# Four residual-and-norm joints of a two-block transformer: two sums of squares in turn, or four sums in one pass

## The chip, the cores and the metric

The kernel runs on one core of a Trainium2 chip, as one program. The metric is device time in microseconds (us) of one execution. Three timed executions of the kernel before took 2606.03, 2606.04 and 2597.53 us, with a median of 2606.03 us. A separate, profiled execution gave the trace from which every row below comes.

## The reference

Two blocks run one after another on 256 latent and 256 context tokens of 1024 features. The first holds two layers (a gated linear attention with grouped attention, then a gated linear recurrence), each followed by a gated feed-forward net; the second holds a latent attention with retention and a state-space layer. What this case is about is the joint between a mixer or a feed-forward net and the norm behind it:

```python
def _rms(x, gain, eps=1e-6):
    y = xf * lax.rsqrt(jnp.mean(xf * xf, axis=-1, keepdims=True) + eps)
    return y * gain

def _modulate(h, shift, scale):
    return h * (1 + scale) + shift

x_lat = x_lat + m_lat[2] * _rms(o_lat @ w_out, norm_post_mix[l])
h_lat = _modulate(_rms(x_lat, norm_pre_ffn[l]), m_lat[3], m_lat[4])
x_lat = x_lat + m_lat[5] * _rms(_swiglu(h_lat, ...), norm_post_ffn[l])
if not last:
    ...   # the same three lines for the context tokens
```

With y the product of a weight and s = m * gain the residual is x + s * y * r, where r is one number per token, the inverse root mean square of y. The next norm needs a second number per token, the inverse root mean square of the new x.

## The kernel before

Features lie on the 128 partitions, in 8 tiles k of 128 features; tokens lie along the free dimension, context tokens first (256), latent tokens behind (256). Each product is three matmuls, because a weight is split into a high part (ACT, line 195) and a low part (DVE, line 196), and so is the normalised input X (high by ACT at line 487, low by DVE at line 492 for even k, and for odd k by ACT at line 489 and POOL at line 490). Lines 205 to 207 are the three matmuls; where 512 tokens pass, the first three weights of a product take context and latent tokens apart, in matmuls of 256 columns.

Four joints have the work in question; the texts call them site 1 to 4:

- site 1: behind the output product of the first mixer (`ew_out`), context and latent;
- site 2: behind the first feed-forward net (`f0_d`), context and latent;
- site 3: behind the output product of the second mixer (`ow_out`), latent alone;
- site 4: behind the second feed-forward net (`f1_d`), latent alone, with the norm for the second block.

At each, and for each of the two token segments, the steps are these. While the product streams, each tile of y is copied out (DVE), squared (ACT, line 70) and summed over its 128 features by a matmul with 32 columns of ones (line 77); tile k writes partitions 32*(k % 4) to 32*(k % 4) + 31 of a PSUM bank (tags pa and pb). At the end the bank is copied (DVE `cp`, line 94), turned to token rows by two matmuls (line 97), and eleven small DVE instructions on 128 x 2 numbers make the inverse root (lines 412 to 420). Two matmuls spread it over partitions again (line 111). Then for 8 tiles DVE forms s * y * r (line 507), POOL or DVE adds it to x (line 508: POOL for k in 0, 1, 3, 4, 6), and the new x is squared and summed like y (lines 70 and 77). A second `cp`, a second turn and a second chain of eleven give the inverse root for the norm, whose 8 tiles follow (lines 486 to 492).

At sites 1 and 2 the last three weights of the product finish their context tokens first, so that the context joint runs beside the latent matmuls.

A scheduler orders each engine's instructions ahead of time; an engine then takes them in that order. Two things besides the joints are put into the same stretches. One is the next block's modulation: 512 KB pieces of `ada_w` are loaded by SP (line 326) into two buffers of the pool `mp` under the tag `mraw`, and PE multiplies them (line 329, two matmuls of 512 columns a piece, to 32-column groups). The other, at site 1, is the preparation of state-space weights: PE spreads small tiles (line 1460), POOL multiplies them (`Ec`, lines 1471 and 1472), PE multiplies the result (line 1479).

## Time and profile before

| what | value |
|---|---|
| timed executions | 2606.03, 2606.04, 2597.53 us |
| profiled execution, its own time | 2601.28 us |
| its span, first to last instruction | 2599.5 us |
| mean granted TensorE clock | 0.962 |
| PE, DVE, ACT, POOL busy | 93%, 58%, 37%, 20% |

The profiled execution lies 4.75 us under the median of the timed ones and inside their spread of 8.5 us. Its own time is 1.8 us more than its span. PE is busy nearly throughout, so a stall of another engine matters only where PE runs out of matmuls that it may do. The four sites are the stretches 415 to 461 us, 895 to 944, 1253 to 1288 and 1474 to 1511.

### The profile page before, as it was taken

The numbers are of one execution on the slowest core, as the hardware profiler recorded it, in microseconds if no ns is written. First come the engines' busy times: TensorE is split into PE (matmuls) and PEld (weight loads), VectorE is DVE, ScalarE is ACT, GpSimd is POOL, SyncE is SP. The second block draws the span as 40 slices with busy tenths as digits, with TensorE's granted clock in tenths as the row PEclk, the third lists the DMA queues.
The fourth block names the chain that finished last, engine by engine and source line by source line (L and its number), as shares of the span: only waits on it lengthen the run. The fifth ranks groups of instructions, "written<-read, shape, count | busy, mean of one in ns | idle before, by whom it ended". The sixth has DMA issues, their size and how long they took to land.

```text
span 2599.5 us, 40143 instructions
## 1 busy us (share of the span) xinstructions
PE 2427.1 (93%) x15813; PEld 1979.1 (76%) x15813; DVE 1513.9 (58%) x2897; ACT 972.1 (37%) x1591; POOL 514.6 (20%) x648
## 2 busy tenths in 40 slices
PE   6999989989889998889999999999999999959999
PEld 5875566768678688889699788556888888628999
DVE  5545436865843466674555552665588744485666
ACT  5523323312222253333444453443423224534443
POOL 2910013763710042330100100110100000260000
PEclk9999999989999999999999999999999999989999
DMA  8326673654543332113665522002365533876564
GB/s 284 116 92 223 242 273 100 166 158 122 153 127 100 104 113 98 59 48 105 255 225 181 194 89 82 17 17 74 111 191 178 170 107 96 185 259 220 154 181 152
DMA packets 162925, 378.05 MB, mean 145 GB/s; under 512 B 24144, under 2 KB 70096, under 8 KB 162608
## 3 DMA queue, kind: packets, MB, share of 16 engines
q1 hardware_dynamic: 159728, 368.27, 44.3%
q0 software_dynamic: 3008, 7.21, 1.4%
q8 instruction: 125, 2.05, 0.3%
q14 instruction: 64, 0.52, 0.1%
HBM read 344.75 MB, written 30.67 MB: 144 GB/s over the span
## 4 chain that ended last, share of the span: by engine, by line
PE 73%; DVE 10%; DMA 6%; POOL 5%; ACT 3%; issue 2%; SPq 1%; POOLq 0%; DVEq 0%; ACTq 0%
PE pl L205 17%; PE pl L206 16%; PE pl L207 16%; PE pm L329 3%; POOL Ec L1471 2%; DMA bc<-s_w 2%; DVE lo L196 2%; PE pl L984 2%; PE pa L77 2%; DMA mcol<-ada_t 1%; POOL Ec L1472 1%; PE pl L279 1%; PE pl L280 1%; PE pl L277 1%; DVE pm L395 1%
## 5 line engine op out<-in xcount | busy, mean ns | idle before, releaser
L195 ACT CAST hi<-raw 128x1024 fp32r<-128x1024 f32 (+4 forms) x393 | 400.2, 1020 | 841.9 <-PE pl L206 640.3
L196 DVE TENSOR_TENSOR lo<-raw,hi 128x1024 fp32r<-128x1024 f32 (+4 forms) x393 | 486.6, 1240 | 341.1 <-ACT hi L195 334.9
L206 PE MATMUL pl<-X,hi 128*128 128x256 f32 (+1 forms) x2032 | 654.2, 323 | 5.9 <-POOL X L490 5.7
L205 PE MATMUL pl<-X,hi 128*128 128x256 f32 (+1 forms) x2032 | 657.6, 326 | 1.6 <-ACT X L487 1.6
L207 PE MATMUL pl<-X,lo 128*128 128x256 f32 (+1 forms) x2032 | 652.1, 322 | 1.5 <-DVE lo L196 1.5
L205 PEld LDWEIGHTS pl<-X,hi 128*128 128x128 f32 x2032 | 395.3, 195 | 39.3 <-issue 9.1
L206 PEld LDWEIGHTS pl<-X,hi 128*128 128x128 f32 x2032 | 395.7, 195 | 37.8 <-POOL X L490 8.6
L207 PEld LDWEIGHTS pl<-X,lo 128*128 128x128 f32 x2032 | 396.2, 195 | 33.4 <-issue 4.9
L205 PE MATMUL pl<-hh,hi 128*128 128x256 f32 (+1 forms) x1071 | 330.0, 309 | 10.7 <-ACT hh L1694 10.6
L206 PE MATMUL pl<-hl,hi 128*128 128x256 f32 (+1 forms) x1071 | 328.4, 307 | 8.5 <-DVE hl L1695 8.3
L207 PE MATMUL pl<-hh,lo 128*128 128x256 f32 (+1 forms) x1071 | 326.8, 306 | 0.0
L205 PEld LDWEIGHTS pl<-hh,hi 128*128 128x128 f32 x1071 | 203.7, 191 | 32.2 <-ACT hh L1694 12.2
L206 PEld LDWEIGHTS pl<-hl,hi 128*128 128x128 f32 x1071 | 204.1, 191 | 20.7 <-DVE hl L1695 10.6
L207 PEld LDWEIGHTS pl<-hh,lo 128*128 128x128 f32 x1071 | 204.4, 191 | 10.4 <-DVE y L1708 0.4
L1471 POOL TENSOR_TENSOR Ec<-PGr,bc 128x576 f32<-128x576 f32 x64 | 102.0, 1609 | 181.4 <-DVE lo L196 84.3
L205 PE MATMUL pl<-M,hi 128*128 128x256 f32 (+1 forms) x416 | 125.9, 305 | 6.9 <-ACT hi L195 5.9
L329 PE MATMUL pm<-mraw,s_cc 128*32 128x512 f32 x576 | 116.0, 606 | 10.3 <-DMA mraw<-ada_w 9.8
L207 PE MATMUL pl<-M,lo 128*128 128x256 f32 (+1 forms) x416 | 123.1, 297 | 1.2 <-DVE lo L196 1.2
L206 PE MATMUL pl<-M,hi 128*128 128x256 f32 (+1 forms) x416 | 123.5, 298 | 0.2 <-DVE M L856 0.2
L1708 DVE TENSOR_TENSOR y<-y,pl 128x256 f32<-128x256 f32 (+1 forms) x86 | 45.2, 526 | 127.2 <-PE pl L207 126.9
L490 POOL TENSOR_TENSOR X<-nt,X 128x256 fp32r<-128x256 f32 x48 | 37.4, 781 | 379.7 <-ACT nt L489 379.7
L395 DVE SCALAR_TENSOR_TENSOR pm<-mcol,mrow 128x512 f32<-128x512 f32 x128 | 89.3, 698 | 36.1 <-DMA mcol<-ada_t 22.4
(515 smaller groups left out, 3757.7 us busy)
## 6 DMA issues: line engine op xcount, KB each, us to landing
mraw<-mod_w SPq DMA_DIRECT2D x96, 512.0 KB, 5.5
raw<-f_u SPq DMA_DIRECT2D x88, 512.0 KB, 3.8
mraw<-ada_w SPq DMA_DIRECT2D x64, 512.0 KB, 6.3
raw<-p_u SPq DMA_DIRECT2D x64, 512.0 KB, 3.6
raw<-p_d SPq DMA_DIRECT2D x64, 512.0 KB, 3.6
raw<-ow_fm SPq DMA_DIRECT2D x32, 512.0 KB, 3.3
mcol<-ada_t SPq DMA_DIRECT2D x64, 256.0 KB, 3.1
raw<-f_d SPq DMA_DIRECT2D x32, 448.0 KB, 3.3
```

The lines of the kernel that those rows point to most:

```text
L77: K.nc.tensor.matmul(self.ps[32 * j:32 * j + 32, :N], K.ones[:rows, :32], self.sq[:rows, :N], start=k < 4, stop=k + 4 >= self.kt, skip_gro ...
L195: nc.scalar.copy(hi, raw)
L196: nc.vector.tensor_tensor(lo, raw, f32(hi), ALU.subtract)
L205: mm(out, w[0][:, kw, wsl], xh, start=first and a == 0, stop=False, skip_group_check=True)
L206: mm(out, w[0][:, kw, wsl], xl, start=False, stop=False, skip_group_check=True)
L207: mm(out, w[1][:, kw, wsl], xh, start=False, stop=last and a == nk - 1, skip_group_check=True)
L329: nc.tensor.matmul(ps[32 * j:32 * j + 32, :], s[:, k, :], raw[:, jj * 512:(jj + 1) * 512], start=k == 0, stop=k == KT - 1, skip_group_chec ...
L395: nc.vector.scalar_tensor_tensor(self.psum("pm"), buf[:, n % 2], 1.0, s[:, v], ALU.mult, ALU.mult, accum_out=(dst if h else part)[:, v, j: ...
L490: nc.gpsimd.tensor_tensor(lo[:, k, a:b], t, f32(hi[:, k, a:b]), ALU.subtract)
L984: nc.tensor.matmul(ps[:, :nk], q[:, tt * P:(tt + 1) * P], k[:, :nk], start=True, stop=True)
L1471: nc.gpsimd.tensor_tensor(Ec[i], ff[i], cs[i], ALU.mult)
L1708: nc.vector.tensor_tensor(y[:, c, a0:b0], y[:, c, a0:b0], ps, ALU.add)
```

## The change

A class `Sums` takes the place of two `Squares` at each of the four sites. As soon as a tile of y is there, it forms four products of 256 tokens: y squared, (s*y) squared, s*y*x and x squared (three by ACT, one by DVE), in one buffer of 4 x 256 numbers, and four matmuls sum them into the four 32-partition groups of one bank, both token segments in the same bank side by side. From the four sums per token the two inverse roots follow: r as before, and the mean square of the new x as S(x,x) + r*(2*S(s*y,x) + r*S(s*y,s*y)), without forming the new x. That chain has eleven, four and eleven small DVE instructions, in one piece. Both roots are spread by four matmuls into one bank, and then each tile gets its residual and, right behind it, its norm. The squares of the new x, their matmuls, the second `cp` and the second turn are gone. In the profile's terms, a segment of a site loses 8 ACT squares and 8 sum matmuls of x and gains 16 ACT squares, 8 DVE products and 24 sum matmuls in the stream of the product. `early` (site 2) puts the context norm beside the latent stream too.

The buffer of `Sums` is taken from the pool `mp` under the tag `mraw`, two buffers.

```diff
+class Sums:
+    def add(self, k, t0, t1):
+        K, nc = self.K, self.K.nc
+        for v, a, b in self.segs:
+            if t0 <= a and b <= t1:
+                self.flush()
+                w = K.mp.tile([P, 4, 256], F32, tag="mraw", name=K.n("sums"), bufs=2)
+                x, y, s = self.x[:, k, a:b], self.y[:, k, a:b], self.Pv[:, v, k:k + 1]
+                nc.scalar.activation(w[:, 0], y, AF.Square)
+                nc.scalar.activation(w[:, 1], y, AF.Square, scale=s)
+                nc.vector.scalar_tensor_tensor(w[:, 2], y, s, x, ALU.mult, ALU.mult)
+                nc.scalar.activation(w[:, 3], x, AF.Square)
+                self.last = w, k, a, b
+    def flush(self):
...
+        for q in range(4):
+            K.nc.tensor.matmul(self.ps[32 * q:32 * q + 32, a:b], K.ones[:, :32], w[:, q], start=first, stop=k == KT - 1,
+                               skip_group_check=True)
+    def rstds(self, i, tag):
...
+        v.tensor_copy(cp[:, :n], self.ps[:, a:b])
+        p2 = K.psum(tag)
+        for t in range(nt):
+            nc.tensor.matmul(p2[:, 4 * t:4 * t + 4], cp[:, t * P:(t + 1) * P], vw(K.ident, 0, [[32, 4]]), start=True,
+                             stop=True)
+        s = [vw(p2, q, [[4, nt]]) for q in range(4)]
...
+        K.rstd_rows(s[0], D, nt, r[0])
+        v.tensor_tensor(u, s[1], r[0], ALU.mult)
+        v.scalar_tensor_tensor(u, s[2], 2.0, u, ALU.mult, ALU.add)
+        v.tensor_tensor(u, u, r[0], ALU.mult)
+        v.tensor_tensor(u, s[3], u, ALU.add)
+        K.rstd_rows(u, D, nt, r[1])
...
-    def halves(self, x, y, accs, vecs):
-        new = self.squares(SEGS)
-        Pv, Av, shift = vecs()
-        c, l = SEGS[:1], SEGS[1:]
-        self.residual_scaled(x, y, Pv, c, [accs[0].rstd()], new)
+    def halves(self, sums, vecs, early):
+        Av, shift = vecs()
+        x = sums.x
+        X = self.norm_tiles(T) if early else None
+        by, bx = sums.rstds(0, "pa")
+        for k in range(KT):
+            self.residual(sums, 0, by, k)
+            if early:
+                self.norm_scaled(X, x, Av, shift, SEGS[:1], [bx], (k,))
         yield
-        bl = accs[1].rstd()
-        bc = new[0].rstd()
-        self.residual_scaled(x, y, Pv, l, [bl], new[1:])
-        X = self.norm_tiles(T)
-        bl = new[1].rstd()
-        self.norm_scaled(X, x, Av, shift, c, [bc])
-        self.norm_scaled(X, x, Av, shift, l, [bl])
+        ly, lx = sums.rstds(1, "pb")
+        if not early:
+            X = self.norm_tiles(T)
+            self.norm_scaled(X, x, Av, shift, SEGS[:1], [bx])
+        for k in range(KT):
+            self.residual(sums, 1, ly, k)
+            self.norm_scaled(X, x, Av, shift, SEGS[1:], [lx], (k,))
         yield X
...
-                acc = K.residual_rms(xl, y, K.vecP(m1[:, :, 2], g[:, 1, 1]), LSEG, acc)
-                X = K.norm_mod(xl, K.vecA(m1[:, :, 4], g[:, 1, 2], "b"), m1[:, :, 3], LSEG, acc)
+                X = K.norm_tiles(LAT)
+                Av = K.vecA(m1[:, :, 4], g[:, 1, 2], "b")
+                by, bx = acc.rstds(0, "pa")
+                for k in range(KT):
+                    K.residual(acc, 0, by, k)
+                    K.norm_scaled(X, xl, Av, m1[:, :, 3], LSEG, [bx], (k,))
```

The scheduler's order changes in several places. In the rows below the line numbers are those of the kernel they come from; the new lines 145, 158, 171, 174 and 188 are the DVE product, the sum matmuls, `cp`, the turn and the spreading of `Sums`; 564 and 565 are the old 507 and 508; 550, 554 and 556 the old 486, 490 and 492; 269 to 271 the old 205 to 207; 390 and 393 the old 326 and 329; 1532, 1533 and 1552 the old 1471, 1472 and 1491.

DVE at site 2, before, where the latent tokens' second copy (cp_7527) stands, after the latent residual and ahead of the context norm (pa_7473 holds the context's inverse root):

```order
L508 TENSOR_TENSOR x<-x,nt_7506 128x256
L507 SCALAR_TENSOR_TENSOR nt_7518<-y_3623,vecP_7277,pb_7449 128x256
L508 TENSOR_TENSOR x<-x,nt_7518 128x256
L94 COPY cp_7527<-pb_7479 128x256
L486 SCALAR_TENSOR_TENSOR nt_7550<-x,vecA_7279,pa_7473 128x256
L412 TENSOR_SCALAR ms_7533<-pb_7529 128x2
L486 SCALAR_TENSOR_TENSOR nt_7554<-x,vecA_7279,pa_7473 128x256
L415 TENSOR_SCALAR ms_7535<-ms_7533 128x2
```

DVE at the same place in the changed kernel, where the latent copy (cp_7603) stands (pa_7445 holds both of the context's inverse roots):

```order
L564 SCALAR_TENSOR_TENSOR nt_7495<-y_3666,vecP_3667,pa_7445 128x256
L550 SCALAR_TENSOR_TENSOR nt_7498<-x,vecA_7397,pa_7445 128x256
L564 SCALAR_TENSOR_TENSOR nt_7502<-y_3666,vecP_3667,pa_7445 128x256
L565 TENSOR_TENSOR x<-x,nt_7502 128x256
L556 SCALAR_TENSOR_TENSOR X_7400<-nt_7498,m_95,X_7399 128x256
L550 SCALAR_TENSOR_TENSOR nt_7505<-x,vecA_7397,pa_7445 128x256
L171 COPY cp_7603<-pa_7043 128x256
L476 TENSOR_SCALAR ms_7610<-pb_7605 128x2
```

Before, the context norm is woven into the latent tokens' second chain; in the changed kernel the latent tokens' only chain of 26 begins behind all 8 context tiles (residual and norm).

PE at site 2, before, from the last sums of y on (mraw are pieces of `ada_w`, rs the inverse roots, pb_7479 the sums of the new x):

```order
L77 MATMUL pb_6996<-sq_7426,ones 32x256
L329 MATMUL pm_7974<-mraw_8095,s_cc_459 32x512
L97 MATMUL pb_7431<-pack_sb,cp_7429 128x1 x2
L97 MATMUL pa_7455<-pack_sb,cp_7453 128x1 x2
L329 MATMUL pm_7974<-mraw_8095,s_cc_459 32x512
L329 MATMUL pm_7974<-mraw_8099,s_cc_459 32x512 x2
L111 MATMUL pb_7449<-pack_sb,rs_7434 128x128 x2
L77 MATMUL pb_7479<-sq_7480,ones 32x256
```

PE at the same place in the changed kernel, from the last sums on:

```order
L158 MATMUL pa_7043<-sums_7594,ones 32x256 x4
L188 MATMUL pa_7445<-pack_sb,rs_7411 128x128 x2
L393 MATMUL pm_8060<-mraw_8061,s_cc_459 32x512
L269 MATMUL pl_7742<-X_7399,hi_7738 128x256
L269 MATMUL pl_7805<-X_7399,hi_7801 128x256
L270 MATMUL pl_7742<-X_7400,hi_7738 128x256
L271 MATMUL pl_7742<-X_7399,lo_7739 128x256
L270 MATMUL pl_7805<-X_7400,hi_7801 128x256
L271 MATMUL pl_7805<-X_7399,lo_7802 128x256
L269 MATMUL pl_7868<-X_7399,hi_7864 128x256
L270 MATMUL pl_7868<-X_7400,hi_7864 128x256
L393 MATMUL pm_8060<-mraw_8061,s_cc_459 32x512
```

Before, six pieces of `ada_w` are worked on in site 1's stretch, six in site 2's and four later. In the changed kernel none is in site 1's; the first of all stands right behind site 2's last sums, twelve of the sixteen are spread among the matmuls of the next three weights (pl_7742, pl_7805, pl_7868), two stand around the fourth weight and two later.

POOL at site 1, before, from the first state-space product behind the first norm tiles (X_3526) on:

```order
L1471 TENSOR_TENSOR Ec_3877<-PGr,bc_3860 128x576
L1472 TENSOR_TENSOR Ec_3876<-Ec_3876,Ec_3877 128x576
L490 TENSOR_TENSOR X_3526<-nt_3582,X_3525 128x256
L1471 TENSOR_TENSOR Ec_3936<-PGr,bc_3860 128x576
L490 TENSOR_TENSOR X_3526<-nt_3591,X_3525 128x256
L1471 TENSOR_TENSOR Ec_3937<-PGr,bc_3860 128x576
L1472 TENSOR_TENSOR Ec_3936<-Ec_3936,Ec_3937 128x576
L490 TENSOR_TENSOR X_3526<-nt_3600,X_3525 128x256
L490 TENSOR_TENSOR X_3526<-nt_3609,X_3525 128x256
L1491 DMA tt<-band_3794 16x8x128
L490 TENSOR_TENSOR X_3526<-nt_3618,X_3525 128x256
```

POOL at site 1 in the changed kernel, up to the last norm tile (nt_3661):

```order
L554 TENSOR_TENSOR X_3569<-nt_3646,X_3568 128x256
L565 TENSOR_TENSOR x<-x,nt_3651 128x256
L1552 DMA tt<-band_3992 16x8x128
L1532 TENSOR_TENSOR Ec_4050<-PGr,bc_4034 128x576
L1532 TENSOR_TENSOR Ec_4051<-PGr,bc_4034 128x576
L1532 TENSOR_TENSOR Ec_4110<-PGr,bc_4034 128x576
L1533 TENSOR_TENSOR Ec_4050<-Ec_4050,Ec_4051 128x576
L1532 TENSOR_TENSOR Ec_4111<-PGr,bc_4034 128x576
L1533 TENSOR_TENSOR Ec_4110<-Ec_4110,Ec_4111 128x576
L1532 TENSOR_TENSOR Ec_4179<-PGr,bc_4163 128x576
L554 TENSOR_TENSOR X_3569<-nt_3661,X_3568 128x256
```

Before, five `Ec` operations stand among the norm tiles. In the changed kernel five stand ahead of the first latent residual tile, and seven more ahead of the last norm tile.

## Rows read from the trace of the kernel before

**Rows 1.** The page: busy time of each engine; the final chain by engine.
```profile
PE 2427.1 (93%) x15813; PEld 1979.1 (76%) x15813; DVE 1513.9 (58%) x2897; ACT 972.1 (37%) x1591; POOL 514.6 (20%) x648
...
PE 73%; DVE 10%; DMA 6%; POOL 5%; ACT 3%; issue 2%; SPq 1%; POOLq 0%; DVEq 0%; ACTq 0%
```

**Rows 2.** One line's instructions: count: ns min/median/max, first and last start.
```profile
L77 PE MATMUL pa<-sq,ones x116: 379/379/617, 400.5 to 1515.1; 128*32 128x256 f32 x114, 128*32 128x512 f32 x2
...
L70 ACT ACTIVATE sq<-y x35: 400/416/420, 414.7 to 1475.2; 128x256 f32<-128x256 f32 x35
...
L508 POOL TENSOR_TENSOR x<-x,nt x30: 721/732/919, 406.2 to 1485.8; 128x256 f32<-128x256 f32 x30
```

**Rows 3.** Timeline of PE, two groups of modulation matmuls: start, us, what, records.
```profile
895.40 1.07 PE L329 MATMUL pm<-mraw,s_cc 128*32 128x512 f32 x8
...
1260.85 1.05 PE L329 MATMUL pm<-mraw,s_cc 128*32 128x512 f32 x4
```

**Rows 4.** Chain of waits: one sum matmul; four state-space ones: start, us, records.
```profile
1249.92 0.43 PE pa L77 x2
...
441.81 0.40 PE pb L1479 x8
```

**Rows 5.** Busy time of each engine in a stretch of site 4.
```profile
1480.00:1490.00 10.00, 10.00 (x48) 4.10 (x47) 4.63 (x11) 2.39 (x6) 3.82 (x5) 1.00 0.95 364
```

**Rows 6.** Timeline of DVE at site 3; in brackets idle time before and its releaser.
```profile
1255.56 0.42 DVE L94 COPY cp<-pa 128x256 f32<-128x256 f32 x1 [1.68 <-PE pa L77]
...
1258.02 1.23 DVE L196 TENSOR_TENSOR lo<-raw,hi 128x1024 fp32r<-128x1024 f32 x1
...
1260.96 1.86 DVE L507 SCALAR_TENSOR_TENSOR nt<-y,vecP,pa 128x256 f32<-128x256 f32 x4 [0.87 <-PE pa L111]
...
1267.86 0.42 DVE L94 COPY cp<-pa 128x256 f32<-128x256 f32 x1 [1.89 <-PE pa L77]
...
1271.97 1.26 DVE L486 SCALAR_TENSOR_TENSOR nt<-x,vecA,pa 128x256 f32<-128x256 f32 x3 [0.87 <-PE pa L111]
```

**Rows 7.** Timeline of POOL and PE at site 3: the last norm tile, a matmul.
```profile
1281.13 0.77 POOL L490 TENSOR_TENSOR X<-nt,X 128x256 fp32r<-128x256 f32 x1 [0.91 <-ACT nt L489]
...
1288.11 0.28 PE L207 MATMUL pl<-X,lo 128*128 128x256 f32 x1
```

**Rows 8.** Busy time, granted clock (behind POOL's) and DMA in a stretch of site 3.
```profile
1280.00:1285.00 5.00, 5.00 (x30) 5.00 (x30) 2.18 (x2) 1.37 (x4) 0.99 (x2) 0.62 0.70 239
```

**Rows 9.** Chain of waits in site 2's stretch.
```profile
895.04 0.31 PE pl L206
...
896.95 4.01 DMA mraw<-ada_w
...
930.13 0.39 PE pl L206
```

**Rows 10.** Timeline of PE, the end of the fourth weight behind site 2.
```profile
943.25 0.50 PE L207 MATMUL pl<-X,lo 128*128 128x512 f32 x2
```

**Rows 11.** DMA issues at site 2: count, KB each, median us to landing.
```profile
mraw<-ada_w SPq DMA_DIRECT2D x6, 512.0 KB, 4.5
```

**Rows 12.** DMA issues, 1220 to 1256 us.
```profile
mraw<-ada_w SPq DMA_DIRECT2D x11, 512.0 KB, 9.9
x<-xd SPq DMA_DIRECT2D x1, 1024.0 KB, 5.9
```

**Rows 13.** The page: DMA issues of the whole run.
```profile
mraw<-ada_w SPq DMA_DIRECT2D x64, 512.0 KB, 6.3
```

**Rows 14.** Timeline of POOL at site 1: state-space product, last norm tile.
```profile
449.99 1.48 POOL L1472 TENSOR_TENSOR Ec<-Ec,Ec 128x576 f32<-128x576 f32 x1
...
454.87 0.75 POOL L490 TENSOR_TENSOR X<-nt,X 128x256 fp32r<-128x256 f32 x1
```

**Rows 15.** Timeline of PE at site 1: the product's last matmul, the fourth weight's first.
```profile
414.82 0.28 PE L207 MATMUL pl<-M,lo 128*128 128x256 f32 x1
...
461.09 0.50 PE L205 MATMUL pl<-X,hi 128*128 128x512 f32 x1
```

More of the change, by code (lines that the diff above doesn't have):

```diff
@@ L493, in norm_scaled @@
                                                    ALU.add, ALU.subtract)
-    def residual_rms(self, x, y, Pv, segs, accs):
-        new = self.squares(segs)
-        self.residual_scaled(x, y, Pv, segs, [acc.rstd() for acc in accs], new)
-        return new
-    def residual_scaled(self, x, y, Pv, segs, bcs, new):
-        nc = self.nc
-        for (v, a, b), bc, acc2 in zip(segs, bcs, new):
-            n = b - a
-            for k in range(KT):
-                t = self.sm.tile([P, 512], F32, tag="nt", name=self.n("nt"), bufs=3)[:, :n]
-                nc.vector.scalar_tensor_tensor(t, y[:, k, a:b], Pv[:, v, k:k + 1], bc[:, :n], ALU.mult, ALU.mult)
-                (nc.gpsimd if k in (0, 1, 3, 4, 6) else nc.vector).tensor_tensor(x[:, k, a:b], x[:, k, a:b], t, ALU.add)
-                acc2.add(x[:, k, a:b])
@@ L1771, in body @@
             K.bg["w"] = K.s5_weights(fp, sc)
-            acc = K.squares(SEGS)
-            step = K.halves(x, y, acc, lambda: (K.vecP(m0[:, :, 5], g[:, 0, 3]), K.vecA(m1[:, :, 1], g[:, 1, 0], "b"),
-                                                m1[:, :, 0]))
+            acc = Sums(K, x, y, K.vecP(m0[:, :, 5], g[:, 0, 3]), SEGS)
+            step = K.halves(acc, lambda: (K.vecA(m1[:, :, 1], g[:, 1, 0], "b"), m1[:, :, 0]), True)
             def half():
@@ L1780, in body @@
             K.ffn(X, 512, A["f0_u"], [A[f"f0_d{i}"] for i in range(3)], "swiglu", y, fp, 9,
-                  lambda k, a, b: K.add_squares(acc, y, k, SEGS, a, b), half=half, ticks=("w", ()))
+                  acc.add, half=half, ticks=("w", ()))
             X = next(step)
@@ L1796, in body @@
                 y = fp.tile([P, KT, LAT], F32, tag="y", name="y0")
-                acc = K.squares(LSEG)
+                acc = Sums(K, xl, y, K.vecP(m1[:, :, 2], g[:, 1, 1]), LSEG)
                 accc = Squares(K, CTX, KT, P, "pb")
@@ L1821, in body @@
                 K.ffn(X, LAT, A["f1_u"], [A[f"f1_d{i}"] for i in range(3)], "swiglu", y, fp, between=context,
-                      after=lambda k, a, b: K.add_squares(acc3, y, k, LSEG, a, b))
-                acc = K.residual_rms(xl, y, K.vecP(m1[:, :, 5], g[:, 1, 3]), LSEG, acc3)
+                      after=acc3.add)
+                by, bx = acc3.rstds(0, "pa")
+                for k in range(KT):
+                    K.residual(acc3, 0, by, k)
+                    K.norm_scaled(X2, x, A2, n0[:, :, 0], SEGS[1:], [bx], (k,))
                 grp[2](pool=fp, bufs=8)
-            K.norm_parts(X2, x, A2, n0[:, :, 0], SEGS[1:], acc)
             nc.sync.dma_start(xd[:, :, CTX:], xl)
```

42 lines of the change are left out of this document (36 added, 6 removed).

## The prediction

> **What bounds the kernel now.** I read the page first. PE is busy 93% of the span, and 73% of the chain that ended last is PE's [rows 1]. So the kernel is PE-bound on the whole, and a shorter joint pays only where PE has run out of matmuls. Then I read the four sites in the table of busy time by stretches, in the timeline and in the chain of waits.
>
> Site 4 never runs out: PE is busy 10.00 of 10 us while the joint runs [rows 5], since the context norm and modulation pieces fill it. There only removed PE work counts. Site 3 is bound by the joint. Its first `cp` starts at 1255.56, the first residual tile at 1260.96, the second `cp` at 1267.86, the first norm tile at 1271.97 [rows 6], and the last norm tile leaves POOL at 1281.9 [rows 7]. Half-fed, PE ran at a granted clock of 0.62 meanwhile [rows 8]. At site 2 the product ends at T0 = 895.35, the chain goes through a 4.01 us load that PE waits for, and the last norm tiles are awaited at 930.13 [rows 9]; the fourth weight ends at 943.75, T0 + 48.4 [rows 10]. At site 1 the product ends at 415.1 and the fourth weight begins at 461.09 [rows 15]; POOL shares itself between norm tiles and `Ec`, and its last norm tile ends at 455.6 [rows 14].
>
> **The sums in the stream.** There are 48 steps (a tile of one segment): 16 at site 1, 16 at site 2, 8 at site 3, 8 at site 4. Before, a step of y has one sum matmul, 0.43 us on PE in two records of 379 ns that overlap [rows 2, 4]. Now it has four, to four column groups. Do they run beside each other? Two modulation matmuls of 512 columns (4 records) took 1.05 us; four (8 records), to four column groups, took 1.07 [rows 3]. So the third and fourth were free, and four sums would cost half of 1.07, 0.535 us, since they have 256 columns: 0.1 us more a step, 5 us for 48. The other bounds: nothing more (0), and one after another, 3 x 0.43 x 48 = 62. Between them, four state-space matmuls of 128 columns took 0.40 [rows 4], where 0.43/2 would be one alone: a factor of 1.9, or 18 us. I take 5, since the modulation matmuls have the same 32-column weights.
>
> The Trainium skill (TensorE: Matmul & The Clock Gate, "Part 3: Packing small matmuls") speaks against the change here: a weight load overlaps matmuls in flight only if its row group differs, and these four sums share all rows. By that rule the four go in turn, the 62 above; rows 3 disagree for equal shapes, so it stays a rival.
>
> The additional squares (16 of 0.42 us a segment [rows 2], before overlap) lie on ACT, at 37% [rows 1], and the DVE products on DVE, at 58%. In the stream they hide behind 24 matmuls a tile; the last tile's three squares lengthen the joint by about two, 0.8 us, at site 3. There x must also be loaded before the stream instead of after it. Its load takes 5.9 us [rows 12], and I allow 2 us of stall for it.
>
> **The new joint.** Its price is worked out once. From the second `cp` to the first norm tile it took 1271.97 - 1267.86 = 4.1 us before [rows 6]: the copy's 0.42, the turns, eleven small instructions, and 0.87 of waiting for the spreading. With 0.6 for the turns the small ones come to 0.2 us each, so fifteen more make it 7.1. Then DVE's tile loop: 16 products and 7 additions or low parts at 0.47 (1.86 for four [rows 6]), 10.8 us, plus the last tile's ACT and POOL, 1.8. POOL's half of it, 5 x 0.73 and 4 x 0.77, lies beside [rows 2, 7]. In sum 19.7 us from the `cp` to the last norm tile. Before, site 3 needed 1281.9 - 1255.6 = 26.3.
>
> **Site 3.** The `cp` starts 0.8 later, at 1256.4. In DVE's new order three weight splits of 1.23 us [rows 6] stand inside the chain; the first covers the turns, two cost 2.5. So the last norm tile is at 1256.4 + 19.7 + 2.5 = 1278.6, less 0.6 for the covered turn: 1278. Before, the first weights were worked on one behind another, and the third ended near 1288.3, 72 matmuls after the first [rows 7]; the new order walks through three weights tile by tile, so 9 matmuls of 0.12 us remain behind the last tile: 1279 to 1280. That is -8 to -9, if no modulation piece stands in the way, and at worst +3, if splits and pieces all come late. With the 2 us stall in the stream and some of these I take **-5**.
>
> **Site 4.** Gone are 8 sums of the new x at 0.43 and one pair of turns at about 0.6: **-4** (between -5 and 0, the latter if fillers merely change place).
>
> **Site 2.** In DVE's new order the latent `cp` stands behind the whole context loop. The context's second root waits for the last y tile, its product and a split (0.42 + 0.48 + 1.23 + two small): T0 + 2.7. The context loop ends at T0 + 13.4, the latent `cp` to last tile takes 19.7: T0 + 33. Nine matmuls and the fourth weight (24 matmuls, under 0.25 us each [rows 10], 5.5 in all) later it is T0 + 39.6 instead of T0 + 48.4: -9 at best. But PE's order now has twelve modulation pieces among those matmuls, the first of them right behind the sums, and two buffers shared with `Sums`, so none can be fetched much before T0. That makes six rounds in turn, each a landing time r plus about 1 us for matmuls in front. The fourth weight then ends at T0 + 6(r + 1) + 6. With r = 4.5, the median here [rows 11], that is T0 + 39, no hindrance; with 6.3, the whole run's [rows 13], T0 + 49.8, 1.4 later than before. I take the middle, **-4**. The pieces that thereby leave site 1 and the later stretch (8 of 16) relieve PE there, where it has gaps anyway: 0.
>
> **Site 1.** The latent joint is shorter here too, but POOL is next: five `Ec` ahead of the first latent residual tile and seven ahead of the last norm tile, 12 x 1.4 = 17 us (1.48 in rows 14), with 5 x 0.73 and 8 x 0.77 of tiles and some 5 us of DMA issue: 32 us of POOL work from about T0 + 6, so T0 + 38 against T0 + 40.5 before. Each `Ec` waits for a PE product in turn. Bounds: -6 if POOL flows freely (the joint's own saving), +6 if two PE waits more end up ahead of the last tile. I take **-2**.
>
> **The sum.** 5 - 2 - 4 - 5 - 4 = -10 us against the profiled execution's 2601.28: 2591.3. That execution lies 4.75 under the median of the timed runs. Since two of three runs stand at 2606 and one at 2597.5, I add half of this difference: **2594 us**.
>
> **The rivals.**
> (A) The forecast, 2586 to 2600 on its own.
> (B) The joints give all they can: sums at no cost, -6, -9, -9 and -4: -28, or 2576 with the same half added. For it speaks the clock, 0.62 at site 3 [rows 8], which has room to rise when PE is fed earlier; against it, the order of POOL and of the pieces.
> (C) It is hidden anyway: what the tails give, the sums take (18 instead of 5 at the middle price): 2601.3 + 18 - 15 = 2604, about 2604 to 2607. For it speaks 93% of PE.
> (D) Slower: PE waits in order for the modulation pieces at site 2. With the landing of 9.9 us that the trace shows where many loads queue [rows 12], the fourth weight ends at T0 + 6 x 10.9 + 6 = T0 + 71, 23 us later than before instead of 4 earlier. With the other terms 2601.3 + 5 - 2 - 5 - 4 + 23 = 2618, 2620 with the half. It decides from r = 6.1, where 6(r + 1) + 6 = 48.4. For it speaks that before, too, PE waited 4.01 us for such a piece at this place [rows 9]; against it, that only two loads are ever in flight there.
> (E) Slower: the four sums go in turn, 62 - 15 = +47, or 2650. Rows 3 speak against it.
>
> **How the numbers follow.** A 0.42, B 0.20, C 0.14, D 0.18, E 0.06. A measurement of this kernel can tell about 0.5%, 13 us, from no change: faster is under 2593, slower over 2619. Half of A and all of B are faster, 0.41; the other half of A, C and a third of D are the same, 0.41; the rest of D and E are slower, 0.18. The range goes from inside B to the near part of D, 2574 to 2622, and leaves out about 0.16.
>
> **What would show it.** The time between the first record of a step's four sums and the next matmul: 0.5 us in A, 1.7 in E. The third weight's end at site 3: near 1280 on the old scale, 8 us earlier in relation to the product's end. At site 2 idle time of PE put down to modulation loads: under 5 us in A, 20 or more in D; the latent `cp` some 13 us behind the product's end. At site 1 the last norm tile behind seven `Ec`, 36 to 40 us behind the product's end. At site 4 PE without a gap, and 4 us less work. It is wrong if the sums cost over 0.2 us a step, if DVE's loop takes much over 11 us because residual and norm of a tile wait for each other through POOL and ACT, or if the wait for x at site 3 stops the stream for more than 2 us.

## The result and the profile after

The changed kernel takes 2617.92 us (median of seven runs, 2615.09 to 2623.85) against 2603.09 for the kernel before (seven runs, 2591.34 to 2611.47). The ratio is 1.0053, with a 95% interval of 1.0034 to 1.0072: some 14 us slower. The forecast was 2594, with a range of 2574 to 2622. The time lies inside the range, the sign was forecast wrong.

The page of the changed kernel, busy time of each engine (before: [rows 1]):

```profile
PE 2416.1 (92%) x15981; PEld 1968.4 (75%) x15981; DVE 1540.6 (59%) x2963; ACT 990.2 (38%) x1640; POOL 510.5 (20%) x648
```

The span is 2615.2 us against 2599.5. PE's busy time fell by 11 us although PE has 168 more instructions. So PE's time without work rose from 172.4 to 199.1, by 27 us: over the whole run the loss is waiting, not busy time. To find where, I measured both traces (and those of the experiments) from the first to the last y tile that DVE writes in each product (at sites 2 and 4 in the last of the feed-forward's products). Change against before, us:

```
stretch                              changed  sites134  sites234  spare12  seg_pend_late
y tiles of site 1                      +5.3     +5.4      +0.0     +4.3      +1.7
up to the feed-forward's first y tile  +0.3     -3.5      -1.2     +2.3      -5.2
y tiles of site 2                      +1.7     +0.3      +1.6     +1.9      -0.9
up to site 3's first y tile           +11.8     -3.9     +11.5     +1.5      -5.9
y tiles of site 3                      +0.0     +0.7      +0.0     +0.0      +0.0
joint of site 3                        -1.1     -1.3      -2.0     -1.6      -0.8
y tiles of site 4                      +0.8     +0.8      +0.8     +0.8      +0.9
```

The last column's kernels are explained with the experiments. The table leaves out what lies between and around its stretches: in the changed kernel -4.6 ahead of site 1, +3.9 inside the first feed-forward and -2.4 in the rest, which with the table's +18.8 makes the 15.7 us of the two spans. Single executions differ by several us in stretches whose code is the same (two kernels with the code of before at site 2 showed -3.9 and, sites34, +3.1 in the fourth row). So only differences that come back in every kernel with the same code are read from this table, like the +4.3 to +5.4 in the first row and the +11.5 to +11.8 in the fourth; smaller ones rest on the timed ratios.

**Site 2** carries the loss. PE's timeline of the changed kernel behind the product, whose last matmul starts at 901.75 (the answer to [rows 9, 10]; in brackets the idle time before and what ended it):

```profile
906.93 1.92 PE L393 MATMUL pm<-mraw,s_cc 128*32 128x512 f32 x2 [1.84 <-DMA mraw<-ada_w]
...
923.90 1.05 PE L393 MATMUL pm<-mraw,s_cc 128*32 128x512 f32 x2 [0.56 <-DMA mraw<-ada_w]
...
930.64 1.92 PE L393 MATMUL pm<-mraw,s_cc 128*32 128x512 f32 x2 [2.59 <-DMA mraw<-ada_w]
...
939.55 1.04 PE L393 MATMUL pm<-mraw,s_cc 128*32 128x512 f32 x2 [1.39 <-DMA mraw<-ada_w]
...
952.25 0.50 PE L269 MATMUL pl<-X,hi 128*128 128x512 f32 x1 [0.54 <-ACT sg L871]
...
957.60 0.39 PE L271 MATMUL pl<-X,lo 128*128 128x512 f32 x1
...
962.51 1.92 PE L393 MATMUL pm<-mraw,s_cc 128*32 128x512 f32 x4 [3.54 <-DMA mraw<-ada_w]
```

The fourth weight begins 50.5 us behind the start of the product's last matmul and ends at T0 + 56; before it was 42.6 and T0 + 48.4. The modulation pieces stand in front of it, five times with a wait for their load, and a sixth wait of 3.54 us follows right behind it: 10.3 us in all, the number that the experiments speak of. What PE waited for up to 958, in sum, and before:

```profile
PE pm L393 <- DMA mraw<-ada_w: 6.8, 5, 2.6
```

```profile
PE pm L329 <- DMA mraw<-ada_w: 0.7, 1, 0.7
```

And the busy time of the pieces' own matmuls in it, changed and before (stretch, sum, PE, weight loads, granted clock, DMA share, GB/s):

```profile
902.00:958.00 56.00, 17.57 (x50) 2.29 (x52) 0.94 0.56 180
```

```profile
895.00:944.00 49.00, 6.55 (x24) 0.99 (x24) 0.93 0.45 147
```

Six microseconds more of waiting, and 11 us more of PE work that stood in other stretches before: 12 to 13 pieces (50 records, four to a piece) are worked on here instead of 6, in 16 groups of two to six records with other matmuls between. A group takes 1.04 to 1.06 us whatever its size; the two behind waits of 1.84 and 2.59 us take 1.92, at a granted clock of 0.50. The fourth weight begins only 7.9 us later, not 17, because PE has less else to do here: the sums take 1.7 us from T0 to the fourth weight instead of 8.7, and PE's other gaps are partly filled. It does not follow that the joint became shorter. Its last norm tile, before and changed, ended on POOL at T0 + 36.2 and T0 + 41.7:

```profile
930.83 0.74 POOL L490 TENSOR_TENSOR X<-nt,X 128x256 fp32r<-128x256 f32 x1 [0.75 <-ACT nt L489]
```

```profile
943.00 0.73 POOL L554 TENSOR_TENSOR X<-nt,X 128x256 fp32r<-128x256 f32 x1 [2.62 <-ACT nt L553]
```

DVE in the same stretch (the residual of a tile is L564, its norm L550, the low part L556):

```profile
905.13 0.48 DVE L564 SCALAR_TENSOR_TENSOR nt<-y,vecP,pa 128x256 f32<-128x256 f32 x1 [0.81 <-PE pa L188]
...
918.79 0.41 DVE L171 COPY cp<-pa 128x256 f32<-128x256 f32 x1
922.22 0.16 DVE L476 TENSOR_SCALAR ms<-pb 128x2 f32<-128x2 f32 x1 [3.01 <-PE pb L174]
...
928.09 0.48 DVE L564 SCALAR_TENSOR_TENSOR nt<-y,vecP,pb 128x256 f32<-128x256 f32 x1 [0.81 <-PE pb L188]
929.40 0.48 DVE L550 SCALAR_TENSOR_TENSOR nt<-x,vecA,pb 128x256 f32<-128x256 f32 x1 [0.83 <-POOL x L565]
929.80 0.47 DVE L564 SCALAR_TENSOR_TENSOR nt<-y,vecP,pb 128x256 f32<-128x256 f32 x1
930.46 0.90 DVE L556 SCALAR_TENSOR_TENSOR X<-nt,m,X 128x256 fp32r<-128x256 f32 x1 [0.18 <-ACT X L551]
```

The latent `cp` stands where it was expected, behind the context loop, but 16.8 us behind the product's end; DVE then waits 3.01 us for its turns, which stand on PE behind 1 us of pieces and 2 us of the product's own matmuls. The loop of the last eight tiles goes from 928.09 to the end of POOL's last norm tile at 943.73. These are 15.6 us, 12.6 were worked out. The rows show two reasons: the norm of a tile waits 0.83 us for the residual that POOL has just added (three tiles of eight), and a low part that starts beside POOL's next residual takes 0.90 us instead of 0.48.

```profile
930.36 0.72 POOL L565 TENSOR_TENSOR x<-x,nt 128x256 f32<-128x256 f32 x1 [0.99 <-DVE nt L564]
```

**Site 1.** PE's sums and DVE's copy of the last y tile (answers to [rows 15]):

```profile
411.28 0.28 PE L271 MATMUL pl<-M,lo 128*128 128x256 f32 x1
411.49 0.64 PE L158 MATMUL pa<-sums,ones 128*32 128x256 f32 x8
416.72 1.47 PE L158 MATMUL pa<-sums,ones 128*32 128x256 f32 x8 [4.60 <-ACT sums L143]
```

```profile
411.36 1.85 DVE L564 SCALAR_TENSOR_TENSOR nt<-y,vecP,pa 128x256 f32<-128x256 f32 x4 [0.94 <-PE pa L188]
...
415.41 0.47 DVE L564 SCALAR_TENSOR_TENSOR nt<-y,vecP,pa 128x256 f32<-128x256 f32 x1
415.80 0.42 DVE L1823 COPY y<-pl 128x256 f32<-128x256 f32 x1
```

The product's last matmul starts at 411.28, but the copy of its tile at 415.80: the context's residual tiles stand ahead of it on DVE. Two roots instead of one come before these tiles, so what was over in time before is now in the way, and PE waits 4.60 us. Of the +5.3 in the table this is the larger part. From the first y copy to the last matmul's start the change is only +1.1 (54.4 instead of 53.3). Later at this site:

```profile
468.77 0.98 POOL L554 TENSOR_TENSOR X<-nt,X 128x256 fp32r<-128x256 f32 x1 [2.89 <-ACT nt L553]
```

```profile
473.43 0.80 PE L269 MATMUL pl<-X,hi 128*128 128x512 f32 x1 [1.34 <-ACT sg L1744]
```

The last norm tile comes at T0 + 58 instead of T0 + 40.5, and the fourth weight begins 62 us behind the product instead of 46 [rows 14, 15]. That is hardly paid: up to the feed-forward's first y tile the change is +0.3, and the tail holds more of the state-space work: in its 62 us DVE was busy 55.3 and POOL 38.8, before 32.8 and 20.6 in 46.

**Sites 3 and 4.** DVE, POOL and PE of the changed kernel at site 3 (answers to [rows 6, 7]; each fence one engine):

```profile
1271.83 0.42 DVE L1860 COPY y<-pl 128x256 f32<-128x256 f32 x1 [3.03 <-PE pl L271]
...
1273.84 0.42 DVE L171 COPY cp<-pa 128x256 f32<-128x256 f32 x1 [1.00 <-PE pa L158]
...
1284.52 0.48 DVE L564 SCALAR_TENSOR_TENSOR nt<-y,vecP,pa 128x256 f32<-128x256 f32 x1 [1.77 <-PE pa L188]
...
1295.51 0.19 DVE L410 TENSOR_TENSOR n<-pm,pack_sb 128x32 f32<-128x32 f32 x1 [1.73 <-PE pm L402]
```

```profile
1301.60 0.72 POOL L554 TENSOR_TENSOR X<-nt,X 128x256 fp32r<-128x256 f32 x1 [2.64 <-ACT nt L553]
```

```profile
1303.06 0.28 PE L271 MATMUL pl<-X,lo 128*128 128x256 f32 x1
```

From `cp` to the first residual tile it takes 10.7 us, where 9.0 were worked out (7.1 + 2.5 - 0.6); `cp` itself starts 2.0 us behind the last y copy instead of the 2.9 assumed. The loop then takes 17.8 instead of 12.6: the same waits for POOL, and once 1.73 us in which DVE stands behind an instruction of the modulation that waits for PE. The last norm tile ends 30.5 us behind the last y copy (28.5 before), the third weight at +31.5 (34.9 before). The granted clock is 1.00 from 1273 to 1303, where it was 0.62 in the stretch of [rows 8]. At site 4 PE has no gap while the joint runs (start, end, sum, PE, weight loads, DVE, ACT, POOL, clock, DMA, GB/s):

```profile
1492.00:1500.00 8.00, 8.00 (x60) 2.84 (x54) 5.99 (x28) 1.34 (x3) 0.00 (x0) 1.00 0.59 193
1500.00:1510.00 10.00, 10.00 (x62) 5.98 (x63) 6.26 (x15) 2.04 (x4) 2.87 (x4) 1.00 0.57 213
```

### The profile page after: what moved, and what is told of

Its sections match the earlier page's. It is cut to its first block, busy times and chain, and to the rows that moved or that the text cites. A ratio compares the mean times of both kernels' runs of the same rounds, so it can differ in the third digit from the quotient of the medians.

```text
span 2615.2 us, 40564 instructions
## 1 busy us (share of the span) xinstructions
PE 2416.1 (92%) x15981; PEld 1968.4 (75%) x15981; DVE 1540.6 (59%) x2963; ACT 990.2 (38%) x1640; POOL 510.5 (20%) x648
## 5 line engine op out<-in xcount | busy, mean ns | idle before, releaser
L270 PE MATMUL pl<-X,hi 128*128 128x256 f32 (+1 forms) x2032 | 650.3, 322 | 10.8 <-DVE X L556 6.2
L269 PE MATMUL pl<-X,hi 128*128 128x256 f32 (+1 forms) x2032 | 647.9, 325 | 6.5 <-ACT X L551 4.6
L269 PEld LDWEIGHTS pl<-hh,hi 128*128 128x128 f32 x1071 | 204.7, 192 | 34.3 <-ACT hh L1755 13.7
L271 PEld LDWEIGHTS pl<-hh,lo 128*128 128x128 f32 x1071 | 205.7, 192 | 10.7 <-issue 1.2
L393 PE MATMUL pm<-mraw,s_cc 128*32 128x512 f32 x576 | 118.9, 608 | 20.6 <-DMA mraw<-ada_w 20.3
```

What stands on the lines that cost most here:

```text
L269: mm(out, w[0][:, kw, wsl], xh, start=first and a == 0, stop=False, skip_group_check=True)
L270: mm(out, w[0][:, kw, wsl], xl, start=False, stop=False, skip_group_check=True)
L271: mm(out, w[1][:, kw, wsl], xh, start=False, stop=last and a == nk - 1, skip_group_check=True)
L393: nc.tensor.matmul(ps[32 * j:32 * j + 32, :], s[:, k, :], raw[:, jj * 512:(jj + 1) * 512], start=k == 0, stop=k == KT - 1, skip_group_chec ...
```

## The experiments

Every ratio is to the kernel before, run beside it on the same chip, with its 95% interval. Times of the experiments are medians; the kernel before stood at 2603 to 2604 beside all of them.

**Which site costs it?** Three kernels put the old code back at some of the sites: the accumulators of before, the old `halves` and `residual_scaled`. `sites134` does it at site 2, `sites234` at site 1, `sites34` at both. The edit at site 2:

```diff
-            acc = Sums(K, x, y, K.vecP(m0[:, :, 5], g[:, 0, 3]), SEGS)
-            step = K.halves(acc, lambda: (K.vecA(m1[:, :, 1], g[:, 1, 0], "b"), m1[:, :, 0]), True)
+            acc = K.squares(SEGS)
+            step = K.halves_old(x, y, acc, lambda: (K.vecP(m0[:, :, 5], g[:, 0, 3]),
+                                                    K.vecA(m1[:, :, 1], g[:, 1, 0], "b"), m1[:, :, 0]))
...
-                  acc.add, half=half, ticks=("w", ()))
+                  lambda k, a, b: K.add_squares(acc, y, k, SEGS, a, b), half=half, ticks=("w", ()))
```

> Only site 2 has the old joint again. Theory L: the pieces' turn at site 2 is gone, 2603 to 2607. Theory S: only a third of the sums is gone, 2610 to 2614.

> Only site 1 has the old joint again. Theory L: the pieces still stand at site 2 behind the sums, so the loss stays but for some 3 us, 2612 to 2617. Theory S: a third of the sums and the first stream's stall of 5 us are gone, 2606 to 2610.

> The new joint only at sites 3 and 4. By the traces, where site 3's tail gained 1.1 us, site 4's 1.6 and site 4's stream lost 0.8: 2 us under the kernel before, within what can be told from it. A rival (the new joint gives at site 3 what was worked out beforehand, and the shift of the loads hid it): 7 to 9 us under it.

Measured: sites134 0.9971 [0.9954, 0.9988]; sites234 1.0010 [0.9995, 1.0026]; sites34 0.9961 [0.9944, 0.9979]. In us: 2595.95, 2606.41 and 2594.00. So the new joint at sites 3 and 4 alone makes the kernel 0.39% (10 us) faster, not the 2 us that the single executions had suggested; the rival's 7 to 9 is nearer. Added to that, site 2 takes back 0.49% (13 us), and site 1 0.10%, which the intervals do not tell from nothing; both together take back 0.92%. The two sum to 0.59%, and the difference is within the intervals too. Read the other way, taking the new joint out of site 1 alone gives 0.43% against the changed kernel, and out of site 2 alone 0.82%. sites134 ended below both of its ranges. sites234 ended in theory S's range, not L's, although the pieces still stand at site 2 there, with 10.3 us of waits and +11.5 in the table: both places cost, site 2 the more. With site 2 as before, PE waits 0.6 us for pieces behind its product.

**Is it the two buffers that `Sums` shares with the pieces?** `spare12` gives `Sums` at sites 1 and 2 two buffers of its own, in tiles that are free there; the order of the pieces changes with it.

```diff
-                w = K.mp.tile([P, 4, 256], F32, tag="mraw", name=K.n("sums"), bufs=2)
+                w = self.room()
...
+        if not self.pairs:
+            for _ in range(2):
+                h, l = (self.pool.tile([P, T], F32R, tag=t, name=K.n("sums"), bufs=9) for t in ("hh", "hl"))
+                self.pairs.append([f32(t)[:, c:c + 256] for t in (h, l) for c in (0, 256)])
+        self.at += 1
+        return self.pairs[self.at % 2]
```

> Sums at sites 1 and 2 takes its two buffers from the feed-forward net's hidden tiles (hh and hl) instead of the pool tag mraw; nothing else is changed by hand. Theory L (the loss is PE waiting in order for modulation pieces whose fetch waits for the two buffers that Sums holds): the pieces go back to site 1 and are fetched early, the 10.3 us of PE waiting for pieces at site 2 fall to under 2, and the kernel comes to 2603 to 2608, about 11 us under the changed kernel. Theory S (the loss is the sums themselves in the streams: PE waiting for their squares, more matmuls): no change against the changed kernel, 2614 to 2619.

Measured: 0.9983 [0.9966, 1.0000] (2599.71 us), 18 us faster than the changed kernel by the two ratios (0.70%): theory L's direction, and more than its 11 us. The pieces now start in site 1's stretch again, and five of them (20 records) are left behind site 2's product. Waits there, and the pieces' work:

```profile
PE pm L406 <- DMA mraw<-ada_w: 2.4, 2, 1.5
```

```profile
900.00:949.00 49.00, 6.08 (x20) 0.95 (x20) 0.79 0.27 84
```

This shows the shared buffers as the cause of the pieces' late place. It does not yet say whether their waits or their work cost the time. And it shows something about the joint itself. The fourth weight begins 47.4 us behind the product's last matmul instead of 50.5, but before the change it was 42.6, with about the same piece work (6.55) in the stretch:

```profile
937.78 0.40 PE L205 MATMUL pl<-X,hi 128*128 128x512 f32 x1
```

```profile
900.25 0.28 PE L284 MATMUL pl<-hh,lo 128*128 128x256 f32 x1
...
947.66 0.80 PE L282 MATMUL pl<-X,hi 128*128 128x512 f32 x1 [2.94 <-ACT sg L884]
```

```profile
942.97 0.72 POOL L567 TENSOR_TENSOR X<-nt,X 128x256 fp32r<-128x256 f32 x1 [2.64 <-ACT nt L566]
```

The last norm tile comes at T0 + 43.2, no earlier than in the changed kernel. So the new joint at site 2 is the longer one even with most pieces elsewhere; by the timed ratios too spare12 (0.9983) is no faster than sites134 (0.9971), which has the old joint there. Behind it comes a wait that the kernel before does not have: the walk ends its three weights together, and PE starts the fourth only when ACT has taken in results of the first (`sg`), 2.94 us later.

**Waits or work?** `noload` keeps the matmuls of the changed kernel and takes the loads away.

```diff
+                if once and k:
+                    raw = kept[h]
+                else:
...
-            K.bg["m"] = K.mods_stream([(s2, A["ada_w"], 0, 0, n0, K.ada_b)])
+            K.bg["m"] = K.mods_stream([(s2, A["ada_w"], 0, 0, n0, K.ada_b)], once=True)
```

> The changed kernel, but of the sixteen modulation pieces of the first group only the first two are fetched, and all 32 matmuls multiply those two: 14 loads of 512 KB are left out, no matmul is, so the modulation is that of other weights. Sums keeps the shared buffers. Theory L (PE waits in order for pieces whose fetch waits for buffers): PE's 10.3 us of waiting for pieces at site 2 fall to under 4, all of them at the first two, and the kernel comes to 2602 to 2608. Rival O (it is the order alone: the 32 matmuls of the pieces themselves, 17 us of PE work, now stand in site 2's tail): still 2612 to 2619.

Measured: 1.0031 [1.0017, 1.0045], 2611.45 us, between the two ranges and nearer O's. In its trace the waits are nearly gone, the work is not:

```profile
PE pm L397 <- DMA mraw<-ada_w: 1.7, 1, 1.7
```

```profile
900.00:958.00 58.00, 13.13 (x64) 2.03 (x64) 0.91 0.25 81
```

The fourth weight still begins 48.6 us behind the product. Of the 18 us that own buffers give back, taking the loads away gives 6, and the intervals of noload and of the changed kernel overlap. But the order moved with the edit: all sixteen pieces now stand in the first 30 us behind the product, in ten groups. So this is no clean test. Nor is the traced execution a typical one: it is the fastest of ten, 2602.13 us where the median is 2611.45. In it the stretch up to site 3's first y tile is +2.2 against before, where the changed kernel had +11.8; so there most of that stretch's loss went with the loads, which speaks for the waits. Where the other executions lose their 9 us no trace shows. How the loss divides between waits and work is not settled.

**Would the old half of `halves` do at site 2?** `spare_late2` is spare12 with the latent sums read ahead of the context's norm (the path of site 1) at site 2.

```diff
-            step = K.halves(acc, lambda: (K.vecA(m1[:, :, 1], g[:, 1, 0], "b"), m1[:, :, 0]), True)
+            step = K.halves(acc, lambda: (K.vecA(m1[:, :, 1], g[:, 1, 0], "b"), m1[:, :, 0]), False)
```

> Own buffers at sites 1 and 2, and at site 2 the context norm no longer early: the latent tokens' copy and chain stand on DVE ahead of the context's norm. If the context loop ahead of the latent chain (13 us on DVE) is what keeps site 2's tail from gaining: 4 to 8 us less than own buffers alone, 2592 to 2596. If PE is covered by the context matmuls meanwhile: no change, 2598 to 2602.

Measured: 0.9960 [0.9944, 0.9975], 2592.30 us, 0.23% less than spare12 and at the edge of its first range; with five executions and intervals that overlap the gain is likely, not certain. The fourth weight begins 43.9 us behind the product instead of 47.4: the latent `cp` no longer stands behind eight context tiles.

**Does the order of the sums matter?** A `Sums` object holds one pending tile; adding a tile issues the sums of the one before, of whichever segment. In the changed kernel the context's sums therefore stand right behind their own squares, and PE waits for them (the stall of 1.66 us in the next row, from site 1's stream):

```profile
363.61 0.64 PE L158 MATMUL pa<-sums,ones 128*32 128x256 f32 x8
...
374.39 1.03 PE L158 MATMUL pa<-sums,ones 128*32 128x256 f32 x8 [1.66 <-ACT sums L143]
```

Three kernels keep one pending tile for each segment, so that sums come one weight later: `pend2` in the changed kernel's buffers, `spare_pend` in those of spare12, `seg_pend` with one own buffer for each segment.

```diff
-                self.flush()
+                self.flush(a)
...
-                self.last = w, k, a, b
+                self.last[a] = w, k, a, b
```

> Own buffers at sites 1 and 2 as before, and each token segment keeps its last tile until its own next one, so that the context's four sums of a tile are not issued in the same step as its squares, but one weight later. If site 1's stream is 5.3 us longer because PE waits in order for squares that are only just made: 3 us come back there, 2595 to 2599. If it is the 48 additional sum matmuls of that stream, at some 0.17 us a step and more: no change against own buffers alone, 2598 to 2602.

> The changed kernel with each segment's sums issued one weight later, but in the buffers shared with the modulation pieces. If the loss at site 2 comes from the shared buffers and is separate from the streams': only the streams' 4 to 7 us come back, 2610 to 2614. If the streams were the cause of it all: 2600 to 2605.

> Own buffers at sites 1 and 2, one per token segment, each segment's sums issued one weight later. (In the earlier run with this delay, spare_pend, a latent tile's buffer was overwritten before it was summed; here it is not, and nothing else is changed.) If the streams' loss was PE waiting in order for squares only just made, the time of that run comes again, 2587 to 2592. If it was fast because of the overwritten buffer's missing wait: 2597 to 2602.

Measured: spare_pend 0.9952 [0.9934, 0.9970]; pend2 1.0015 [0.9998, 1.0032]; seg_pend 0.9952 [0.9931, 0.9972]. In spare_pend a buffer of the last latent tiles is written again before it is summed, so its latent sums are of other numbers; seg_pend has the same order without that, and the same time. The pending tile is worth 0.31% with own buffers and 0.38% with the shared ones. In us: 2589.26 (under its range, so more came back than the 3 us asked for), 2608.32 (between its two ranges) and 2591.23 (as expected for waits on squares). In seg_pend_late, which has it, sums of two segments stand together and no sums inside the stream of site 1 wait for squares; only the last ones, behind the product, still wait 3.4 us:

```profile
367.35 1.07 PE L170 MATMUL pa<-sums,ones 128*32 128x256 f32 x16
```

**All three.** `seg_pend_late` is seg_pend with the edit of spare_late2.

> The same with the context norm of site 2 not early. Taken alone that gave 0.23% against own buffers. If the two gains are of different stretches (streams, and site 2's tail), they add up: 2582 to 2587. If both only free the same wait at site 2: as seg_pend, 2587 to 2592.

Measured: 0.9928 [0.9901, 0.9954], 2583.95 us. It beats the kernel before by 0.7% (19 us) and the changed one by 1.2%. That is inside the range for two gains that add up, but 0.24% under seg_pend is no more than the two intervals allow by chance. Behind site 2's product, whose last matmul starts at 890.45, the fourth weight begins after 41.2 us, with 2.7 us of waits for pieces:

```profile
931.60 0.50 PE L280 MATMUL pl<-X,hi 128*128 128x512 f32 x1 [2.94 <-ACT sg L882]
```

**What holds the loop at 17.8 us?** `sites34_dve` is sites34 with all residual adds on DVE; `seg_pend_late_sq` is seg_pend_late with the residual's product in another pair of buffers than the norm's.

```diff
-        (nc.gpsimd if k in (0, 1, 3, 4, 6) else nc.vector).tensor_tensor(x[:, k, a:b], x[:, k, a:b], t, ALU.add)
+        nc.vector.tensor_tensor(x[:, k, a:b], x[:, k, a:b], t, ALU.add)
```

```diff
-        t = self.sm.tile([P, 512], F32, tag="nt", name=self.n("nt"), bufs=3)[:, :b - a]
+        t = self.sm.tile([P, 512], F32, tag="sq", name=self.n("nt"), bufs=2)[:, :b - a]
```

> The new joint at sites 3 and 4 alone, with every residual addition on DVE instead of five of eight on POOL. At site 3 the tile loop took 17.8 us from the first product to the last norm tile, where 12.6 were worked out. If that is the way of a tile through POOL and back: the loop falls to 13 to 14 us, and the kernel to 2588 to 2591. If DVE's own work or ACT sets the loop: no change or up to 2 us more, 2593 to 2597.

> As seg_pend_late, and the residual's product goes to the two buffers of the squares (tag sq) instead of sharing three (tag nt) with the norm. If the tile loop (17.8 us at site 3 where 12.6 were worked out) is held by those three buffers: the loop falls to 13 to 15 us and 3 to 6 us come off at sites 3 and 4, 2577 to 2583. If the way of each tile through DVE, POOL and ACT holds it: no change against seg_pend_late.

Measured: sites34_dve 0.9989 [0.9977, 1.0002], seg_pend_late_sq 0.9970 [0.9951, 0.9989]: 2600.96 and 2594.29 us, both slower than the kernel they are made from and outside all of their ranges, and the loop at site 3 is 17.1 us in both. Without POOL's adds the waits for POOL are gone, but DVE has five more adds, and one wait for the modulation has grown:

```profile
1274.43 0.19 DVE L410 TENSOR_TENSOR n<-pm,pack_sb 128x32 f32<-128x32 f32 x1 [2.96 <-PE pm L402]
```

Without this wait sites34_dve's loop would be 14.1 us, and sites34's, with its wait of 1.73, 16.1; so by this estimate POOL's adds cost some 2 us of the loop. But neither they nor the shared buffers hold it alone. seg_pend_late_sq lost 13 us at another place than the edit's target, between site 1 and the feed-forward (+7.9 against -5.2 in the table's second row), where PE now waits for POOL's state-space products:

```profile
PE pb L1551 <- POOL Ec L1544: 3.3, 1, 3.3
```

In seg_pend_late these waits are 0.8 us. I did not look further for what moved them.

## Why the prediction was wrong, point by point

**Site 2, forecast -4: the steps that failed.** Measured are 12 us more up to site 3, and 0.49% by the timed kernels. Two terms failed, the path of the joint and the price of the pieces. The first is the joint's own path, worked out to end at T0 + 33 and so to give 9 at best. Its last norm tile ended at T0 + 41.7. The context loop took 13.7 us where 10.7 were worked out, from `cp` to the first latent tile it was 9.3 instead of 7.1, and the latent loop took 15.6 instead of 12.6. The waits between DVE, POOL and ACT and the wait for the turns had no price in the sum. The pieces are not the reason: with most of them elsewhere, in spare12, the last tile came at T0 + 43.2. So the order of this joint had no gain to give at site 2.

The second term is the formula for the pieces, T0 + 6(r + 1) + 6. With r = 4.5 it gave T0 + 39, no hindrance, and the forecast was taken in the middle between that and r = 6.3. The landing was 4.5 indeed, but the fourth weight ended at T0 + 56. The formula let the rounds of loads run beside the joint, as if PE were free for whichever was ready; but PE took its matmuls in order, so what stood behind a piece waited with it, 10.3 us in six waits. And it allowed about 1 us of matmuls a round, 6 in all, where the pieces' groups took 17.6 us. Four of these groups stood between the last norm tile and the fourth weight. The sentence "The pieces that thereby leave site 1 and the later stretch (8 of 16) relieve PE there, where it has gaps anyway: 0" looked only at what they leave, not at what they cost where they arrive.

**Rival D** had the place, the sign and, with 2618 to 2620, the time. Its mechanism was right in part only: loads do not take 9.9 us there, the median landing in this stretch is 4.5 us as before (the row below), and the fourth weight came 8 us later, not 23. The rest of its price came from places that it did not name, site 1 and the stretch behind the fourth weight, with its wait of 3.54 us. That its time agrees is partly chance. Its argument that PE had waited 4.01 us for a piece before was a misreading: that is the load's length in the chain, and PE, which had sums to do meanwhile, stood idle for 0.7.

```profile
mraw<-ada_w SPq DMA_DIRECT2D x14, 512.0 KB, 4.5
```

**The sums in the stream, forecast +5.** The likely value was about right. With +1.1 at site 1 (up to the last matmul) and +1.7, 0 and +0.8 at the others (table) it is 3.6 in sum. From the first of a step's sums to the next product matmul it is mostly 0.57 us for four (363.61 above, and below). Before it was 0.55 for one sum alone and 0.99 for the two segments' sums together (380.69 to 381.68). That makes 0.02 to 0.08 us a step, where 0.1 was forecast. At site 1 the wait of 1.66 us for squares stands in the stream too, which had no term; and the pending tile gives back 0.31 to 0.38%, more than these stretches show, so the order of the sums costs in other places as well.

```profile
364.18 0.38 PE L269 MATMUL pl<-M,hi 128*128 128x256 f32 x1
```

```profile
380.69 0.62 PE L77 MATMUL pa<-sq,ones 128*32 128x256 f32 x2
...
381.68 0.50 PE L205 MATMUL pl<-M,hi 128*128 128x512 f32 x1
...
391.43 0.62 PE L77 MATMUL pa<-sq,ones 128*32 128x256 f32 x2
391.98 0.38 PE L205 MATMUL pl<-M,hi 128*128 128x256 f32 x1
```

Eight records of four sums take 0.64 us. The prediction took the sentence on weight loads in the Trainium skill (TensorE: Matmul & The Clock Gate, "Part 3: Packing small matmuls") to mean that they go in turn, 1.7 us. The same section's table of measured speedups has 2.38 times for three column tiles, so the section does not mean that. The trace agrees with the table, as [rows 3] did, and rival E falls.

**Site 1, forecast -2.** It cost 0.10%, 2.6 us, with site 2 as before, which is not clear of noise, and 0.43%, 11 us, beside the new site 2; why the two differ stays open. The step that failed is the T0: I took the product's end as given, and the context's residual tiles moved ahead of the last y copy (4.5 us). The last norm tile at T0 + 58, 20 us later than the T0 + 38 worked out for POOL, did not matter: other work filled the time.

**Site 3, forecast -5, measured about -1 in single executions.** The 2 us stall for x did not come (0.0 in the table), and the first residual tile came 12.7 us behind the last y copy, 0.8 later than worked out. The loop was mis-sized: 12.6 us forecast, 17.8 measured, with 1.73 of it a wait for the modulation. It was named as what would make the prediction wrong, "residual and norm of a tile wait for each other through POOL and ACT", and the price was not in the sum. The walk through three weights tile by tile did what was expected of it: the third weight ends 1.0 us behind the last norm tile, where it was some 6 before, and that makes up for the later tile. Part of this may be the clock: those last matmuls ran at 0.62 before [rows 8] and at 1.00 now, as rival B had hoped. (PE is busy for 5.00 of 5.00 us in [rows 8]; the prediction's "half-fed" fits the 10 us before it, where PE was busy for 6.4.)

**Site 4, forecast -4.** PE never lacks work while the joint runs, as forecast, and sites 3 and 4 together give 10 us by the timed kernel sites34. In single executions I can find only part of it there, so how it divides between the two stays open.

**The clock** had no term in the sum. Its mean is 0.959 in the traced execution against 0.962 before, and 0.958 against 0.962 over all timed ones. In the 92 executions of the kernel before that ran beside the experiments, a mean lower by 0.001 went with 1.7 us more; so by this estimate some 7 of the 14 us go with the lower clock. At 0.959 and 0.960 the kernel before took 2602 to 2618 us, 2607 on average. Whether the lower clock comes of PE's waits or stands beside them no run shows; after two of the waits at site 2 the trace has it at 0.50.

## What to carry to other kernels

When a change borrows a buffer, look at who else fills it: the borrower's life decides where the next load is issued, and on an engine that works in order the matmuls behind that load move too, with their waits and with their own work. Price moved filler at the place where it arrives, not only where it leaves. And when residual and norm of one tile are put behind each other, count each hand-over between engines in the loop: eight tiles with hand-overs took 15.6 to 17.8 us here (the longest with a wait of 1.73 for other work), where the sum of the instructions was 12.6.

## What had not been expected of the hardware

Modulation matmuls to different column groups run beside each other so fully that two records take 1.04 us, six 1.06 (below) and eight 1.07 [rows 3]. Where the order sets them apart, as behind site 2 in the changed kernel, each group pays the full microsecond.

```profile
925.52 1.06 PE L393 MATMUL pm<-mraw,s_cc 128*32 128x512 f32 x6
...
949.24 1.04 PE L393 MATMUL pm<-mraw,s_cc 128*32 128x512 f32 x2
```

A low part on DVE of 0.48 us took 0.90 to 0.98 when it started beside a residual add on POOL, while a norm product of DVE that started at 936.31 beside POOL's norm tile of 936.29 stayed at 0.48. The two differ on both engines, and no run separates what of that matters.
